# Batch norm with ReLU: the first load of x in four strided parts, and the parameter vectors read through the gpsimd queue

## The chip, the core and the metric

The kernel runs on one core of one Trainium2 chip, written in Bass with the Tile framework. The metric is the device time of one execution in microseconds. The kernel before takes 83.73 us, the median of three runs (83.72 to 83.98).

## The reference

Inference-mode batch normalisation of x with shape (32, 128, 32, 32) in float32, followed by ReLU:

```python
normalized = (x - running_mean[None, :, None, None]) / np.sqrt(running_var[None, :, None, None] + eps)
scaled = normalized * gamma[None, :, None, None] + beta[None, :, None, None]
return np.maximum(scaled, 0).astype(np.float32)
```

x is 16.78 MB and the result is as large. The four parameter vectors have 128 floats each; eps is the constant 1e-5. Since the statistics are given, each channel needs one scale and one bias, and each element one multiply, one add and one maximum.

## The kernel before

**Tiling.** Batch and channel are put together into 4,096 rows of 1,024 floats (one image of one channel, 4 KB). A block t (there are two) is 128 partitions times J = 16 rows: partition p of block t holds rows 2048 t + 16 p to 2048 t + 16 p + 15. So a partition holds 16 neighbouring channels, and scale and bias are tables of 128 x 16. The j-th row of a partition uses column j of these tables.

**Pieces.** Each block is cut along j into pieces (PIECES, line 16): for block 0 rows 0-1, 2-3, 4-7 and 8-15, for block 1 rows 0-7 and 8-15. A piece is one tile of its own and is loaded by one transfer (line 52) of 128 partitions, each of which receives one contiguous stretch of 8, 16 or 32 KB. All pieces have their own buffer; x fits into SBUF whole, and no load waits for a buffer to come free. The six loads are issued by SP (SyncE), in the order of the pieces.

**Parameters.** Four transfers, issued by ACT (line 59), put the four vectors into `raw`, 8 partitions x 4 x 16 floats, 64 bytes per partition and vector. POOL writes a 0/1 matrix `rep` (lines 63 and 64: memset, then affine_select), and one matrix product (line 74) spreads the 8 partitions over 128, into `cols` in PSUM. ACT takes the square root of the variance plus eps (line 82), and DVE makes the reciprocal, the scale and the bias (lines 84 to 90).

**Main loop.** ACT goes through the pieces (lines 93 to 108): for each row j one activation of 128 x 1,024 with ReLU, scale and bias (line 96), in place. After the last row of a piece, and after row 0 of the first piece (STORE_CUTS), ACT issues the store of what is finished (line 104). There are 7 stores: two of 0.5 MB, then 1, 2, 4, 4 and 4 MB.

**What sets the order.** Each engine executes its instructions in the program's order; the main loop's order on ACT is the written one. Transfers issued by SP and by ACT go through one queue each. Tile gives each of these transfers one of eight completion semaphores, in turn, and when a transfer takes over a semaphore that an earlier one used, its issuing engine first waits until the earlier one has landed. In the kernel before, the fourth load of x (rows 8-15 of block 0) takes over the semaphore of running_var, the fifth that of running_mean, and the sixth that of the second piece of x.

Of the kernel before, what the change touches and what calls it, by code (L numbers as in the profile page):

```python
# [1 line left out]

# [4 lines left out]


F32 = mybir.dt.float32
ACTF = mybir.ActivationFunctionType  # L10

J = 16

PIECES = (((0, 2), (2, 4), (4, 8), (8, 16)), ((0, 8), (8, 16)))

STORE_CUTS = {(0, 1)}


@with_exitstack
def kernel(
    ctx: ExitStack,
    tc: tile.TileContext,
    x: bass.AP,
    gamma: bass.AP,
    beta: bass.AP,
    running_mean: bass.AP,
    running_var: bass.AP,
    eps: bass.AP,  # L30
    out: bass.AP,
):
    nc = tc.nc
    B, C, H, W = x.shape
    HW = H * W
    P = nc.NUM_PARTITIONS
    assert C % J == 0 and P % (C // J) == 0 and (B * C) % (P * J) == 0
    Q = C // J
    T = B * C // (P * J)

    xr = x.rearrange("b c h w -> (b c) (h w)").rearrange("(t p j) w -> t p j w", p=P, j=J)
    outr = out.rearrange("b c h w -> (b c) (h w)").rearrange("(t p j) w -> t p j w", p=P, j=J)

    data = ctx.enter_context(tc.tile_pool(name="data", bufs=1))
    params = ctx.enter_context(tc.tile_pool(name="params", bufs=1))
    psum = ctx.enter_context(tc.tile_pool(name="psum", bufs=1, space=bass.MemoryType.PSUM))

    tiles = []
    for t in range(T):
        for a, b in PIECES[t]:  # L50
            xt = data.tile([P, b - a, HW], F32, name=f"x{t}_{a}")
            nc.sync.dma_start(out=xt, in_=xr[t, :, a:b, :])  # L52
            tiles.append((t, a, b, xt))

    raw = params.tile([Q, 4, J], F32, name="raw")
    for k, src in enumerate((running_var, gamma, running_mean, beta)):
        nc.scalar.dma_start(out=raw[:, k, :], in_=src.rearrange("(q j) -> q j", j=J))
    eps_t = params.tile([P, 1], F32, name="eps_t")  # L60
    nc.vector.memset(eps_t, float(eps))  # L61
    rep = params.tile([Q, P // Q, Q], F32, name="rep")
    nc.gpsimd.memset(rep, 1.0)  # L63
    nc.gpsimd.affine_select(  # L64
        out=rep,
        in_=rep,
        compare_op=mybir.AluOpType.is_equal,
        fill=0.0,
        base=0,
        pattern=[[0, P // Q], [-1, Q]],  # L70
        channel_multiplier=1,
    )
    cols = psum.tile([P, 4, J], F32, name="cols")
    nc.tensor.matmul(  # L74
        cols.rearrange("p k j -> p (k j)"),
        rep.rearrange("q r s -> q (r s)"),
        raw.rearrange("q k j -> q (k j)"),
        start=True,
        stop=True,
    )  # L80
    std_t = params.tile([P, J], F32, name="std_t")
    nc.scalar.activation(out=std_t, in_=cols[:, 0, :], func=ACTF.Sqrt, bias=eps_t[:, 0:1], scale=1.0)  # L82
    rstd_t = params.tile([P, J], F32, name="rstd_t")
    nc.vector.reciprocal(out=rstd_t, in_=std_t)  # L84
    scale_t = params.tile([P, J], F32, name="scale_t")
    nc.vector.tensor_mul(out=scale_t, in0=cols[:, 1, :], in1=rstd_t)  # L86
    ms_t = params.tile([P, J], F32, name="ms_t")
    nc.vector.tensor_mul(out=ms_t, in0=cols[:, 2, :], in1=scale_t)  # L88
    bias_t = params.tile([P, J], F32, name="bias_t")
    nc.vector.tensor_sub(out=bias_t, in0=cols[:, 3, :], in1=ms_t)  # L90

    with tc.manual_schedule(engines={mybir.EngineType.Activation}):
        for t, a, b, xt in tiles:
            first = a
            for j in range(a, b):
                nc.scalar.activation(  # L96
                    out=xt[:, j - a, :],
                    in_=xt[:, j - a, :],
                    func=ACTF.Relu,
                    bias=bias_t[:, j : j + 1],  # L100
                    scale=scale_t[:, j : j + 1],
                )
                if j + 1 == b or (t, j + 1) in STORE_CUTS:
                    nc.scalar.dma_start(
                        out=outr[t, :, first : j + 1, :], in_=xt[:, first - a : j + 1 - a, :]
                    )
                    first = j + 1


# [1 line left out]
_INS = ['x', 'gamma', 'beta', 'running_mean', 'running_var', 'eps']  # L111
_OUTS = [((32, 128, 32, 32), 'float32')]

_NUMBERS = {'eps': 1e-05}


# [26 lines left out]
```

## Time and profile before

| what | us |
|---|---|
| median of the runs shown | 83.73 |
| the profiled execution | 83.77 |
| its span, first to last instruction | 81.9 |
| ACT busy in the span (34 instructions) | 38.5 |
| PE, DVE and POOL busy, each | below 1 |
| first ReLU starts | 9.72 |
| last ReLU ends, and the last store is issued | 55.97 |
| load and store packets' time, each, on 16 DMA engines | 48.4% and 47.8% of the span |

The span counts from the core's first instruction to its last. The rest of the execution's time lies before and after it. DMA issues are listed as instructions of the engine that issues them (SPq, ACTq); the time given there is that of the issue, and not that of the transfer, which the DMA engines carry out later. A releaser ("<-") is what ended an engine's idle time. In tables by window, the last columns are the granted TensorE clock, the mean busy share of the 16 DMA engines (it can pass 1, as a packet is counted where it starts), and the GB/s that they moved.

### The profile page before, as it was taken

What the parts mean: (1) busy time and instruction counts of PE and PEld (TensorE: products, weight loads), DVE (VectorE), ACT (ScalarE), POOL (GpSimd) and SP (SyncE); (2) the same over time, 40 slices, a digit from 0 to 9 for tenths busy, and PEclk for the clock granted to TensorE, in tenths of its full rate; (3) what the DMA queues carried; (4) which work ended last, traced back from release to release, by engine and by line L of the source; (5) the groups of instructions that cost most, each with busy time, mean ns of one, the idle gap of its engine ahead of it and who ended that gap; (6) DMA issues with size and microseconds to landing.
All of it is one profiled execution on the core that took longest, in us unless ns stands there. A gap on an engine that the chain in (4) does not pass through costs nothing.

```text
span 81.9 us, 119 instructions
## 1 busy us (share of the span) xinstructions
PE 0.7 (1%) x2; PEld 0.5 (1%) x2; DVE 0.8 (1%) x5; ACT 38.5 (47%) x34; POOL 0.8 (1%) x6
## 2 busy tenths in 40 slices
PE   0002000000000000000000000000000000000000
PEld 0002000000000000000000000000000000000000
DVE  0000300000000000000000000000000000000000
ACT  0600377799039999199994199993000000000000
POOL 3000000000000000000000000000000000000000
DMA  2899999989899999979789798996999899799690
GB/s 32 328 425 472 408 448 448 512 352 494 370 448 416 446 418 396 500 296 600 320 380 580 304 464 384 512 512 288 480 512 400 368 512 448 320 512 496 272 512 0
DMA packets 1936, 33.56 MB, mean 410 GB/s; under 512 B 272, under 2 KB 272, under 8 KB 528
## 3 DMA queue, kind: packets, MB, share of 16 engines
q1 hardware_dynamic: 864, 16.78, 48.4%
q10 hardware_dynamic: 1072, 16.78, 47.8%
HBM read 16.78 MB, written 16.78 MB: 410 GB/s over the span
## 4 chain that ended last, share of the span: by engine, by line
DMA 56%; ACT 11%; SPq 0%; issue 0%
DMA x<-in_x_dram 56%; ACT x L96 11%; SPq L52 0%
## 5 line engine op out<-in xcount | busy, mean ns | idle before, releaser
L96 ACT ACTIVATE x<-x,bias_t,scale_t 128x1024 f32<-128x1024 f32 x32 | 37.0, 1228 | 10.3 <-DMA x<-in_x_dram 7.9
L82 ACT ACT_TABLE_LOAD x1 | 1.3, 1283 | 2.6 <-issue 2.6
L82 ACT ACTIVATE std_t<-cols,eps_t 128x16 f32<-128x16 f32 x1 | 0.3, 273 | 4.5 <-PE cols L74 4.5
L74 PE MATMUL cols<-raw,rep 8*128 8x64 f32 x2 | 0.7, 428 | 7.7 <-DMA raw<-in_beta_dram 7.7
L74 PEld LDWEIGHTS cols<-raw,rep 8*128 8x128 f32 x2 | 0.5, 304 | 7.7 <-issue 7.7
L64 POOL TENSOR_SCALAR_AFFINE_SELECT rep<-rep 8x128 f32<-8x128 f32 x1 | 0.4, 392 | 0.1
L84 DVE RECIPROCAL rstd_t<-std_t 128x16 f32<-128x16 f32 x1 | 0.3, 254 | 7.8 <-ACT std_t L82 7.8
L63 POOL MEMSET rep<- 8x128 f32 x1 | 0.2, 195 | 0.3 <-POOLq L124 0.3
L86 DVE TENSOR_TENSOR scale_t<-cols,rstd_t 128x16 f32<-128x16 f32 x1 | 0.2, 175 | 0.1
L90 DVE TENSOR_TENSOR bias_t<-cols,ms_t 128x16 f32<-128x16 f32 x1 | 0.2, 175 | 0.0
L88 DVE TENSOR_TENSOR ms_t<-cols,scale_t 128x16 f32<-128x16 f32 x1 | 0.2, 175 | 0.0
L124 POOL MEMSET const-bfloat16-1.0<- 128x1 bf16 x1 | 0.1, 106 | 0.0
L124 POOL MEMSET const-uint8-127<- 128x1 uint8 x1 | 0.1, 106 | 0.0
L124 POOL MEMSET const-float32-0.0<- 128x1 f32 x1 | 0.1, 103 | 0.3 <-issue 0.3
L124 POOL MEMSET const-float32-1.0<- 128x1 f32 x1 | 0.1, 103 | 0.0
L61 DVE MEMSET eps_t<- 128x1 f32 x1 | 0.1, 59 | 0.9 <-PEq L124 0.9
## 6 DMA issues: line engine op xcount, KB each, us to landing
x<-in_x_dram SPq DMA_DIRECT2D x3, 4096.0 KB, 38.8
out_dram<-x ACTq DMA_DIRECT2D x3, 4096.0 KB, 27.9
x<-in_x_dram SPq DMA_DIRECT2D x2, 1024.0 KB, 5.7
x<-in_x_dram SPq DMA_DIRECT2D x1, 2048.0 KB, 11.2
out_dram<-x ACTq DMA_DIRECT2D x1, 2048.0 KB
out_dram<-x ACTq DMA_DIRECT2D x2, 512.0 KB, 18.8
out_dram<-x ACTq DMA_DIRECT2D x1, 1024.0 KB
raw<-in_running_var_dram ACTq DMA_DIRECT2D x1, 0.5 KB
```

What stands on the lines that cost most here:

```text
L61: nc.vector.memset(eps_t, float(eps))
L63: nc.gpsimd.memset(rep, 1.0)
L64: nc.gpsimd.affine_select(out=rep, in_=rep, compare_op=mybir.AluOpType.is_equal, fill=0.0, base=0, pattern=[[0, P // Q], [-1, Q]], channel ...
L74: nc.tensor.matmul(cols.rearrange("p k j -> p (k j)"), rep.rearrange("q r s -> q (r s)"), raw.rearrange("q k j -> q (k j)"), start=True, s ...
L82: nc.scalar.activation(out=std_t, in_=cols[:, 0, :], func=ACTF.Sqrt, bias=eps_t[:, 0:1], scale=1.0)
L84: nc.vector.reciprocal(out=rstd_t, in_=std_t)
L86: nc.vector.tensor_mul(out=scale_t, in0=cols[:, 1, :], in1=rstd_t)
L88: nc.vector.tensor_mul(out=ms_t, in0=cols[:, 2, :], in1=scale_t)
L90: nc.vector.tensor_sub(out=bias_t, in0=cols[:, 3, :], in1=ms_t)
L96: nc.scalar.activation(out=xt[:, j - a, :], in_=xt[:, j - a, :], func=ACTF.Relu, bias=bias_t[:, j : j + 1], scale=scale_t[:, j : j + 1],)
L124: nc = _bacc.Bacc("TRN2", target_bir_lowering=False, num_devices=1)
```

## The change

Two things change.

The first piece of x (block 0, rows 0-1) is loaded by four transfers instead of one. Transfer s takes partitions s, s + 4, s + 8 and so on: 32 partitions with 8 KB each. All four write to the same tile, with a semaphore each, and SP issues them one after the other ahead of the other five loads, which are as before. The first ReLU now waits for all four.

The four parameter vectors are read by transfers that POOL (GpSimd) issues instead of ACT. They stand on POOL ahead of the memset and the affine_select that make `rep`, and use completion semaphores of a kind of their own. With the transfers that remain on SP and ACT, the eight semaphores are now handed round differently: the fourth load of x takes over that of the first of the four transfers, the fifth that of the last of the four, and the sixth that of the first store.

```diff
 STORE_CUTS = {(0, 1)}
+
+SEED = 4
...
             xt = data.tile([P, b - a, HW], F32, name=f"x{t}_{a}")
-            nc.sync.dma_start(out=xt, in_=xr[t, :, a:b, :])
+
+            n = SEED if (t, a) == (0, 0) else 1
+            for s in range(n):
+                nc.sync.dma_start(out=xt[s::n], in_=xr[t, s::n, a:b, :])
             tiles.append((t, a, b, xt))
...
     raw = params.tile([Q, 4, J], F32, name="raw")
     for k, src in enumerate((running_var, gamma, running_mean, beta)):
-        nc.scalar.dma_start(out=raw[:, k, :], in_=src.rearrange("(q j) -> q j", j=J))
+        nc.gpsimd.dma_start(out=raw[:, k, :], in_=src.rearrange("(q j) -> q j", j=J))
```

## The prediction

> **What bounds the kernel now.** I read the slices and the queue totals first, then the chain of waits, then the waits of SP's own queue, and last the windows and the timeline of the first microseconds.
>
> ```profile
> DMA  2899999989899999979789798996999899799690
> ACT  0600377799039999199994199993000000000000
> ...
> q1 hardware_dynamic: 864, 16.78, 48.4%
> q10 hardware_dynamic: 1072, 16.78, 47.8%
> ...
> DMA x<-in_x_dram 56%; ACT x L96 11%; SPq L52 0%
> L96 ACT ACTIVATE x<-x,bias_t,scale_t 128x1024 f32<-128x1024 f32 x32 | 37.0, 1228 | 10.3 <-DMA x<-in_x_dram 7.9
> ```
>
> The 16 DMA engines are busy in every slice from the second on, with loads (q1) and stores (q10) taking half each. ACT works 37.0 of 81.9 us, waits for x, and is done long before the end. The chain names loads and ACT only because it is followed from instructions; after its last entry the DMA engines still drain stores. So this is a byte stream of 33.56 MB with a head and a tail.
>
> ```profile
> 0.00:1.50 1.50, 0.00 (x0) 0.00 (x0) 0.06 (x1) 0.00 (x0) 0.80 (x6) 1.00 0.00 0
> 1.80:1.90 0.10, 0.00 (x0) 0.00 (x0) 0.00 (x0) 0.00 (x0) 0.00 (x0) 1.00 2.35 329
> 1.90:2.00 0.10, 0.00 (x0) 0.00 (x0) 0.00 (x0) 0.00 (x0) 0.00 (x0) 1.00 1.60 246
> 2.00:2.50 0.50, 0.00 (x0) 0.00 (x0) 0.00 (x0) 0.00 (x0) 0.00 (x0) 1.00 0.60 131
> 2.50:3.00 0.50, 0.00 (x0) 0.00 (x0) 0.00 (x0) 0.38 (x1) 0.00 (x0) 1.00 0.77 311
> 4.00:5.00 1.00, 0.00 (x0) 0.00 (x0) 0.00 (x0) 0.00 (x0) 0.00 (x0) 1.00 1.01 418
> 60.00:80.00 20.00, 0.00 (x0) 0.00 (x0) 0.00 (x0) 0.00 (x0) 0.00 (x0) 1.00 0.98 421
> 80.30:80.60 0.30, 0.00 (x0) 0.00 (x0) 0.00 (x0) 0.00 (x0) 0.00 (x0) 1.00 0.02 0
> ```
>
> (Windows; the last two columns are the DMA share and GB/s, bytes counted where their packet starts.) x starts at 1.8 us, the flow is even near 420 GB/s from 3 us, with loads alone, mixed, or stores alone, and ends at about 80.45. From 1.8 to 3.0 us, 33 + 25 + 66 + 156 = 280 KB move; at 426 GB/s it would be 511 KB. That lack of 231 KB is 0.54 us of ramp. So the profiled run of 83.77 us is: 1.8 before the first bytes, 0.54 of ramp, 78.1 of stream (33.56 MB at 430 GB/s), 1.45 of completions and closing barrier in the span, 1.87 outside it. It is 0.04 above the median of 83.73, so I carry sums over unchanged.
>
> ```profile
> SPq L52 <- DMA raw<-in_running_mean_dram: 4.1, 1, 4.1
> ...
> 0.81 0.59 ACTq L59 DMA_DIRECT2D raw<-in_running_var_dram  x1
> 1.43 0.29 ACTq L59 DMA_DIRECT2D raw<-in_gamma_dram  x1
> ...
> 10.99 0.38 ACTq L104 DMA_DIRECT2D out_dram<-x  x1
> ```
>
> SP's fifth load waited 4.1 us, since completion semaphores are handed round among eight and it takes over the one of a parameter. While SP and ACT both issue, the first parameter issue takes 0.59 us against 0.29 for the next.
>
> **What the Trainium skill says.** "DMA: Bandwidth & Descriptors", section "Issuing engines are not separate DMA queues": transfers of all issuing engines run on the same 16 DMA engines and interleave. The trace agrees: 418 GB/s with loads alone, 421 with stores alone. Same page, "The descriptor swizzle": in a 128-partition transfer each DMA engine writes the partitions of one SBUF port; for other shapes it only says that the outer size decides how many engines take part. "SBUF — State Buffer", section "Door 1: The DMA port swizzle": four neighbouring partitions share a port, ports repeat after 32, and 1 MiB over 8 ports ran at 189 GB/s against 328 over all 16. "DMA: Bandwidth & Descriptors", "Latency and other measured facts": first byte about 0.6 us from SP or ACT, about 1 us from gpsimd. Here SP's first issue begins at 0.81 and bytes start at 1.8; ports and gpsimd transfers are in no run before.
>
> **The change part by part.**
>
> *Parameters off ACT's queue.* ACT loses four issues (0.59 + 0.29 + 0.31 + 0.45 = 1.64 us), and its table load moves from 2.6 to about 1 us. Nothing waits for that: ACT is next needed when the matmul is done at 8.4. It frees the start for SP: the first parameter's packets stand just ahead of x. Worth 0 to 0.1 us at the head.
>
> *Parameters onto POOL's queue.* Four issues now stand ahead of the memset of rep (0.20 us) and its affine_select (0.39). At an estimated 1 us each, from the skill's first-byte figure, they run from 0.8 to 4.8, and rep, ready at 1.5 before, is ready near 5.6. The tiny packets then take turns with x's rows, as they did before, when the last parameter let the matmul start at 7.73. I put the matmul at 6 to 12 us, so first ReLU at 8 to 14 instead of 9.72. Cost on the end: 0. What hides it is the backlog: loads alone are 16.78 / 0.426 = 39.4 us of DMA work. The cover ends where the last store comes too late: ACT needs 56.31 - 9.72 - 7.9 (its waits for loads) = 38.7 us, the last store of 4.19 MB 9.85 us, so first ReLU may be as late as 80.45 - 9.85 - 38.7 = 31.9.
>
> *The semaphores move along.* The built order shows that in the new kernel the fourth load of x waits for seed 0, the fifth for seed 3, and the sixth (the last) for the first store. That store was issued at 10.99 and landed 14.2 us later, at 25.2; the last load was issued at 7.99 before and will be at about 25 to 30. Queued behind it on SP: nothing but the closing waits. It costs 0, because the fifth load keeps its queue busy until ACT gets it at 34.8: 5 to 9 us of cover; past that, stores of 1 to 4 MB stand in the other queue and the engines stay busy.
>
> *Four transfers for one.* Each moves 32 rows of 8 KB, 2 per DMA engine. SP's issues took 328 to 678 ns, median 398; three more are 1.2 us of SP. Per seed an engine has 2 rows of 8 KB at 418/16 GB/s, 0.63 us of work, so issue keeps ahead and the later loads are still early. 48 more completion packets are 3 per engine: under 0.1 us. At the head, fewer rows are made ready before all 16 engines have one: worth from 0 to the ramp's 0.54 us. I take 0.1, because even with descriptors at hand a first row has to come from HBM, and nothing in the trace says that the ramp is descriptor generation.
>
> *Ports.* This is the term that decides. Every fourth partition reaches all 16 ports, but what counts is which engine takes which rows. If 32 rows are dealt out so that each engine keeps a port of its own, the price is 0. If they are dealt out in plain order, two rows each, engine e takes partitions 8e+s and 8e+4+s, two neighbouring ports, and engine e+4 takes the same two (32 partitions on). Two engines then always work through the same pair of ports in the same order. In step, each gets half: 8 rows x 0.31 us (8 KB at 26 GB/s) = 2.5 us becomes 5.0. Every DMA engine has a fixed share of bytes, so the slowest pair sets the end. Bounds 0 to +2.5. The skill describes the port-by-port deal for 128 partitions only, so I take plain order as likelier, and 2.0 of the 2.5, since engines start up to a row apart and partly miss each other.
>
> Sum: 83.77 + 2.0 (ports) - 0.15 (head) = 85.6.
>
> **The rivals.** (A) Forecast: ports shared while the seeds load; 85.6, own range 84.6 to 86.2. For it: no layout for 32 rows is promised, and the skill's 189 against 328 GB/s says that half the ports carry about half the rate. Against: no run shows it. (B) No change: engines keep a port each, the ramp stays; 83.7, 83.5 to 83.95. For it: everything else hides under the stream. (C) Faster, by one mechanism: the ramp of 0.54 us is the time in which 128 rows' descriptors are made, and 32 rows need a quarter, 0.54 x 3/4 = 0.4 us earlier; 83.35. For it: SP's first issue shares the start with ACT's, and engines begin over 1.8 to 2.5 us. It shows as a gain from 0.25 us, and needs unshared ports. (D) POOL gets slow enough to matter, first ReLU after 31.9: each microsecond beyond costs one; it would take parameters five times later than now.
>
> **How the numbers follow.** A 0.50, B 0.24, C 0.21, D and small losses (issue slower than 0.63 us per seed, closing work for the gpsimd queue) 0.05, near 84.1. About 0.3%, 0.25 us, is what a measurement here can tell from none. Faster 0.21, same 0.24, slower 0.55. The range is 83.2 to 86.2: C down to its likely end, A up to full sharing with the head gained; outside it lie the full ramp gain and sharing that spreads to the second load.
>
> **What would show it.** Right: x's first piece lands about 2 us later (at 5.5 us before: 4.7, the shortest landing of an x load, after its issue at 0.81), the GB/s between 2 and 7 us near 210 to 300 instead of 420, then the same stream, ending 2 us later; first ReLU anywhere from 8 to 14 us without moving the end; SP's last load issued near 25 to 30 us. Wrong: 420 GB/s from 2.5 or 3 us on would mean ports are not shared, and the time is B's or C's by where the ramp begins; holes in the slices between 35 and 80 us would mean that a store or the late load does matter.

## The result, and the profile after

The changed kernel takes 86.69 us (median; 86.44 to 87.24), the kernel before beside it 83.77. The ratio is 1.0347, 95% interval 1.0314 to 1.0380: 2.9 us slower, where 1.9 us were forecast and 2.4 us was the upper end of the range. The profiled execution took 86.67 us with a span of 85.0, which is 3.1 more than before.

The slices and queue totals of the kernel after, from its page:

```profile
DMA  0989999999999999999999899999999999999950
GB/s 0 294 274 355 420 417 501 411 417 417 417 411 442 417 447 422 415 419 459 432 436 440 378 428 478 455 432 417 447 432 432 447 417 432 447 432 417 432 216 0
...
q1 hardware_dynamic: 912, 16.78, 48.0%
q10 hardware_dynamic: 1008, 16.78, 46.0%
...
L101 ACT ACTIVATE x<-x,bias_t,scale_t 128x1024 f32<-128x1024 f32 x32 | 37.0, 1228 | 13.2 <-DMA x<-in_x_dram 10.9
```

The same bytes in the same two queues, the same 37.0 us of activations: still a byte stream. What is new stands at the ends of the second row. Slices of 2.1 us carry 294, 274 and 355 GB/s before the stream reaches 420, and the slice before last carries 216. In between it runs as before.

Windows show it more finely. The kernel after (last two columns: mean busy share of the DMA engines, GB/s):

```profile
2.00:3.00 1.00, 0.00 (x0) 0.00 (x0) 0.00 (x0) 0.31 (x1) 1.00 (x3) 1.00 0.87 246
3.00:4.00 1.00, 0.00 (x0) 0.00 (x0) 0.00 (x0) 0.00 (x0) 0.93 (x4) 1.00 1.01 345
4.00:6.00 2.00, 0.00 (x0) 0.00 (x0) 0.00 (x0) 0.00 (x0) 0.19 (x1) 1.00 0.78 246
6.00:10.00 4.00, 0.66 (x2) 0.50 (x2) 0.18 (x1) 0.27 (x1) 0.00 (x0) 1.00 1.03 377
80.00:81.00 1.00, 0.00 (x0) 0.00 (x0) 0.00 (x0) 0.00 (x0) 0.00 (x0) 1.00 0.99 426
81.00:82.00 1.00, 0.00 (x0) 0.00 (x0) 0.00 (x0) 0.00 (x0) 0.00 (x0) 1.00 0.69 295
82.00:83.00 1.00, 0.00 (x0) 0.00 (x0) 0.00 (x0) 0.00 (x0) 0.00 (x0) 1.00 0.08 33
```

The same windows of the kernel before:

```profile
2.00:3.00 1.00, 0.00 (x0) 0.00 (x0) 0.00 (x0) 0.38 (x1) 0.00 (x0) 1.00 0.69 221
3.00:4.00 1.00, 0.00 (x0) 0.00 (x0) 0.00 (x0) 0.90 (x1) 0.00 (x0) 1.00 1.01 426
4.00:6.00 2.00, 0.00 (x0) 0.00 (x0) 0.00 (x0) 0.00 (x0) 0.00 (x0) 1.00 1.01 418
6.00:10.00 4.00, 0.65 (x2) 0.49 (x2) 0.78 (x4) 0.55 (x2) 0.00 (x0) 1.00 1.07 455
```

Two things are to be seen. Between 4 and 6 us the engines move 246 GB/s instead of 418, and their busy share is 0.78: they are partly *idle*. Engines that share ports would be busy at a low rate (e6 below shows that picture), so the forecast's mechanism is in doubt from this line on. And the end is ragged: the share falls from 0.99 over 0.69 to 0.08 within three microseconds, so the engines no longer finish together.

The trace also holds a record of each DMA packet: its queue, start, duration and bytes, but not its engine. A packet of x carries one partition's contiguous stretch, called a row from here on. Each load and store ends with 16 packets of 4 bytes, read here as one completion mark per engine (96 for the six loads of the kernel before).

These records give both sizes. By the marks of the last store, the stream is 1.89 us behind that of the kernel before when it ends, on the mean of the 16 engines (82.32 us against 80.43), and the last engine ends 1.41 us after that mean (83.73), against 0.18 before (80.61). So 1.89 us of lag and 1.23 us of straggling make the 3.1 us of span.

The lag is made in the first 10 us: counted in bytes it is 0.25 us at 4 us, 1.08 at 6 and 1.70 at 10, and from 16 us on it stays between 1.8 and 2.0. From 4 to 10 us the mean engine is idle for 0.33 us, nearly all of it before 6 us, and slow rows take 0.9 us per engine more than their normal time. So the slow rows are the larger part, and more than half of that time (0.57 us) belongs to rows begun after 6 us, when the engines hardly idle any more.

The straggling begins at the head, too. For the piece of rows 4-7 the engines put down their completion marks over 2.5 us (13.4 to 15.9), for the piece of 4 MB after it again over 2.5 us (24.5 to 26.9), and they end over 2.1 us. Before, the first two of these spreads are 0.3 and 0.4 us. A spread that arose in the first microseconds is still there at the last store. That it is the same engine throughout is likely, but the records don't show it.

The issues of x by SP, up to 4.4 us (shortest, median, longest in ns). Before, then after:

```profile
L52 SPq DMA_DIRECT2D x<-in_x_dram x4: 372/426/678, 0.8 to 2.2; - x4
```

```profile
L57 SPq DMA_DIRECT2D x<-in_x_dram x6: 432/578/594, 0.8 to 3.9; - x6
```

A strided seed costs SP 0.54 to 0.59 us instead of about 0.42, so one goes out every 0.62 us. A seed is 0.62 us of work for the 16 engines (two rows of 8 KB each at 0.309 us). The queue gets its next work just when the last is done, and nothing is in hand. The first row of x begins at 2.13 us instead of 1.84.

The parameters' side, in the timeline of the kernel after:

```profile
1.33 0.67 POOL L64 DMA_DIRECT2D raw<-in_running_var_dram  x1 [0.81 <-POOLq L129]
...
3.01 0.52 POOL L64 DMA_DIRECT2D raw<-in_beta_dram  x1
3.52 0.20 POOL L68 MEMSET rep<- 8x128 f32 x1
3.79 0.40 POOL L69 TENSOR_SCALAR_AFFINE_SELECT rep<-rep 8x128 f32<-8x128 f32 x1
...
10.81 1.24 ACT L101 ACTIVATE x<-x,bias_t,scale_t 128x1024 f32<-128x1024 f32 x1 [1.02 <-DVE bias_t L95]
```

and SP's waits:

```profile
SPq L57 <- DMA out_dram<-x: 17.9, 1, 17.9
SPq L57 <- DMA x<-in_x_dram: 4.0, 1, 4.0
```

POOL issues the four in 0.67 + 3 x 0.52 us and has `rep` ready at 4.2. The matrix product then waits for the last parameter, which lands at 8.7, and the first ReLU starts at 10.81. SP's last load waits 17.9 us for the first store, is issued at 27.1, and no slice between 35 and 80 us is low.

### The profile page after: what moved, and what is told of

Its sections match the earlier page's. It is cut to its first block, busy times and chain, and to the rows that moved or that the text cites. A ratio compares the mean times of both kernels' runs of the same rounds, so it can differ in the third digit from the quotient of the medians.

```text
span 85.0 us, 123 instructions
## 1 busy us (share of the span) xinstructions
PE 0.7 (1%) x2; PEld 0.5 (1%) x2; DVE 0.8 (1%) x5; ACT 38.5 (45%) x34; POOL 3.0 (4%) x10
## 4 chain that ended last, share of the span: by engine, by line
DMA 52%; ACT 11%; issue 3%; POOL 2%; DVE 1%; PE 1%; DVEq 0%; POOLq 0%
DMA x<-in_x_dram 28%; DMA out_dram<-x 18%; ACT x L101 11%; DMA raw<-in_beta_dram 7%; POOL raw L64 2%; PE cols L79 1%; ACT std_t L87 0%; DVE rstd_t L89 0%; DVE ms_t L93 0%; DVE scale_t L91 0%; DVE bias_t L95 0%; DVEq L91 0%; POOLq L129 0%
## 5 line engine op out<-in xcount | busy, mean ns | idle before, releaser
L64 POOL DMA_DIRECT2D raw<-in_running_var_dram x1 | 0.7, 672 | 0.8 <-POOLq L129 0.8
L64 POOL DMA_DIRECT2D raw<-in_gamma_dram x1 | 0.5, 518 | 0.0
L64 POOL DMA_DIRECT2D raw<-in_running_mean_dram x1 | 0.5, 518 | 0.0
L64 POOL DMA_DIRECT2D raw<-in_beta_dram x1 | 0.5, 518 | 0.0
```

The source lines that it names most:

```text
L64: nc.gpsimd.dma_start(out=raw[:, k, :], in_=src.rearrange("(q j) -> q j", j=J))
```

## The experiments

Theories at the outset. *Ports*: two engines share a port pair while seeds load, and each row takes up to twice as long. *Supply*: the seeds come too slowly or too small for one queue, engines run dry, and rows take their normal time. *Parameters*: the gpsimd queue and the later first store have a price. In most kernels below the four parameter reads are left out and `raw` is filled with constants, so that only the loads of x differ; this is called "no parameter reads". Its edit is the first one shown. All ratios are to the kernel before on the same chip, with the 95% interval.

### No parameter reads, first piece whole (e1)

```diff
-    for k, src in enumerate((running_var, gamma, running_mean, beta)):
-        nc.scalar.dma_start(out=raw[:, k, :], in_=src.rearrange("(q j) -> q j", j=J))
+    nc.vector.memset(raw[:, 0:2, :], 1.0)
+    nc.vector.memset(raw[:, 2:4, :], 0.0)
```

> The kernel before without any parameter transfer: raw is filled with ones (variance, gamma) and zeros (mean, beta) by DVE, so the reading of the four vectors is left out. It is the base for the two other kernels without parameter transfers. Three theories stand against each other for the loss of 2.9 us. Ports: two DMA engines share SBUF ports in a strided transfer of 32 partitions, which so runs at about half the rate. Issue: such a transfer takes SP longer to issue (0.54 to 0.59 us in the changed kernel against 0.37 to 0.43), and the engines run out of rows. Gpsimd: the parameter transfers of POOL hold up the DMA engines or SP's issues. All three expect 83.4 to 83.9 us here, as the parameters are hidden.

84.12 us, 1.0032 (1.0020 to 1.0043). It is the base for the kernels below, and by itself a surprise: without any parameter transfer, and with the first ReLU at 5.71 us instead of 9.72, it is not faster but 0.3% slower. The packet records put the loss at 9 to 12 us (0.3 us) and 40 to 50 us (0.2 us), where loads and earlier stores mix and some rows are slow; the start is as before.

### The four seeds alone (e2), and the gpsimd queue alone (e3)

e2 is e1 with the change's four strided transfers:

```diff
-            nc.sync.dma_start(out=xt, in_=xr[t, :, a:b, :])
+            n = SEED if (t, a) == (0, 0) else 1
+            for s in range(n):
+                nc.sync.dma_start(out=xt[s::n], in_=xr[t, s::n, a:b, :])
```

e3 is the kernel before with the other half of the change:

```diff
-        nc.scalar.dma_start(out=raw[:, k, :], in_=src.rearrange("(q j) -> q j", j=J))
+        nc.gpsimd.dma_start(out=raw[:, k, :], in_=src.rearrange("(q j) -> q j", j=J))
```

> The first piece in four strided transfers, and no parameter transfer at all (raw filled by DVE as in the base, the reading of the four vectors is left out). Ports and issue: 2 to 3 us above the base, 85.7 to 86.8. Gpsimd: within 0.3 us of the base, 83.4 to 84.0. If SP's issues are slow because of their shape they still take 0.54 to 0.59 us; if POOL made them slow they take 0.33 to 0.43.

> The kernel before with the second half of the change alone: parameters read by the gpsimd queue, the first piece in one transfer. Ports and issue: no change, 83.5 to 84.0. Gpsimd: most of the loss, 85.2 to 86.7, with SP's first issues at 0.54 us or more and fewer than 16 engines busy between 4 and 6 us.

e2: 86.49 us, 1.0313 (1.0288 to 1.0337), or 2.81% over e1. e3: 84.36 us, 1.0055 (1.0030 to 1.0079), above the range without a price (83.5 to 84.0) and far under that of the gpsimd theory. The two add up to 3.36% against the change's 3.47%, well inside its interval. So about five sixths of the loss belong to the seeds. The windows of e2 repeat the pattern of the kernel after, though POOL issues nothing here:

```profile
4.00:6.00 2.00, 0.00 (x0) 0.00 (x0) 0.00 (x0) 0.00 (x0) 0.00 (x0) 1.00 0.79 258
6.00:10.00 4.00, 0.00 (x0) 0.00 (x0) 0.00 (x0) 1.38 (x2) 0.00 (x0) 1.00 1.01 346
```

Share 0.79, so idle engines again. Of the 22 rows of 8 KB that began between 3.5 and 4.0 us, 15 took 0.309 us, the time of an undisturbed row; ports shared by pairs of engines would show in all of them. The slowest rows (0.7 to 1.2 us) come from 4 us on, beside the idling and for two microseconds after it.

### Strided transfers where the queue is full (e5)

e2's edit, moved from the first piece to the 4 MB piece of rows 8-15 of block 0 (the condition is `(t, a) == (0, 8)`); the first piece is whole. The seeds have the same 32 partitions, with 32 KB each.

> No parameter transfer (raw filled by DVE, the reading of the four vectors is left out), the first piece whole, and instead the piece of rows 8 to 15 of block 0 (4.19 MB) in four strided transfers of 32 partitions with 32 KB each. SP issues them while the engines still have the pieces before to load, and each holds 2.5 us of work. Ports: these 4.19 MB run at half the rate, 9.8 us become up to 19.7, and the time is 88 to 94. Issue: within 0.5 us of the base, 83.4 to 84.3. Gpsimd: the same as issue.

84.01 us, 1.0024 (1.0016 to 1.0033): not slower than e1. In the stretch in which most of these rows are loaded it moved

```profile
12.00:25.00 13.00, 0.00 (x0) 0.00 (x0) 0.00 (x0) 4.63 (x4) 0.00 (x0) 1.00 1.06 452
```

and e1, with the whole transfer,

```profile
12.00:25.00 13.00, 0.00 (x0) 0.00 (x0) 0.00 (x0) 4.79 (x5) 0.00 (x0) 1.00 1.02 438
```

If every fourth partition made engines share ports, these 4 MB, 9.8 us of work at 426 GB/s, would take up to twice as long. They run at full rate: all 128 rows of 32 KB took 1.21 us, the time of such rows in the kernel before. The ports theory falls for strided seeds. SP's last load goes out only at 27.7 us here, as late as in the changed kernel, so that lateness isn't the loss either.

### Neighbouring partitions instead (e6)

As e2, with transfer s taking the 32 neighbouring partitions from 32 s on.

```diff
-                nc.sync.dma_start(out=xt[s::n], in_=xr[t, s::n, a:b, :])
+                q = P // n
+                nc.sync.dma_start(out=xt[s * q : s * q + q], in_=xr[t, s * q : s * q + q, a:b, :])
```

> No parameter transfers (raw filled by DVE; the reading of the four vectors is left out), the first piece in four transfers of 32 neighbouring partitions, 0 to 31, 32 to 63 and so on. Three theories for the 2.4 us that the four strided transfers cost without any parameter transfer. Supply: SP hands out one of them every 0.62 us, just what 16 engines load in that time (2 rows of 8 KB each), so engines run out of rows, and a row that starts on an idle engine takes 0.5 to 1 us instead of 0.31. Deal: rows of a strided transfer are dealt out so that engines get in each other's way, and the packets are slow for that. Count: three more small transfers cost by themselves, whatever their shape. Supply: SP's issues show whether the stride makes them slow: 85.8 to 86.8 if they still take 0.53 to 0.59 us, 83.9 to 84.6 if they take 0.43 or less. Deal: another time, 88 or more if neighbours make it worse, under 84.6 if better. Count: as the strided ones, 86.2 to 86.8.

85.36 us, 1.0169 (1.0143 to 1.0195), outside all the ranges: SP's issues were fast (0.38 to 0.43 us), but there is another cost. Here the ports do show:

```profile
3.00:4.00 1.00, 0.00 (x0) 0.00 (x0) 0.52 (x3) 0.00 (x0) 0.00 (x0) 1.00 1.05 229
4.00:6.00 2.00, 0.00 (x0) 0.00 (x0) 0.00 (x0) 0.00 (x0) 0.00 (x0) 1.00 1.08 238
```

The engines are busy throughout (share 1.05 to 1.08) and move 229 to 238 GB/s. All 13 rows that began between 3.5 and 4.0 us took 0.62 to 0.64 us, twice 0.309. The Trainium skill ("SBUF — State Buffer", "Door 1: The DMA port swizzle") says that 32 neighbouring partitions reach 8 of 16 ports, with 189 against 328 GB/s for 1 MiB; that is a ratio of 0.58, and the trace's 0.56 (238 of 426) agrees. This is what a shared port looks like. Such a doubling of every row isn't in the traces of the change.

### All partitions, a quarter of the columns each (e7)

As e2, with transfers of 128 partitions and 2 KB:

```diff
-            for s in range(n):
-                nc.sync.dma_start(out=xt[s::n], in_=xr[t, s::n, a:b, :])
+            if n > 1:
+                for s in range(n):
+                    j, c = s // 2, (s % 2) * (HW // 2)
+                    nc.sync.dma_start(out=xt[:, j, c : c + HW // 2], in_=xr[t, :, j, c : c + HW // 2])
+            else:
+                nc.sync.dma_start(out=xt, in_=xr[t, :, a:b, :])
```

> No parameter transfers (raw filled by DVE; the reading of the four vectors is left out), the first piece in four transfers of all 128 partitions with 2 KB each: the same 256 KB per transfer, in the shape of a whole load. Supply: issues of 0.37 to 0.43 us every 0.47 us stay ahead of 0.62 us of work, 83.9 to 84.6. Deal: no loss, 83.9 to 84.4. Count: 86 to 86.8.

85.35 us, 1.0168 (1.0127 to 1.0209). No stride, no shared port. SP's issues are fast, and the first row begins at 1.80:

```profile
L59 SPq DMA_DIRECT2D x<-in_x_dram x4: 366/422/432, 0.8 to 2.2; - x4
```

They go out every 0.47 us for 0.67 us of work each (per engine eight rows of 2 KB at 0.084 us). Yet the engines run dry at the same place:

```profile
4.00:6.00 2.00, 0.00 (x0) 0.00 (x0) 0.00 (x0) 1.24 (x1) 0.00 (x0) 1.00 0.89 286
```

So slow issue is not the whole cause, and the supply theory as it stood (83.9 to 84.6) missed: four transfers of 256 KB on one queue lose 1.1 us (1.36% over e1) even when SP is ahead. Slow rows stand beside the idling here too, although these transfers have no stride.

### A bigger first piece (e8), and seeds on two queues (e9)

e8 makes the first piece of four rows instead of two (PIECES of block 0: 0-3, 4-7, 8-15), so each strided seed has 1.2 us of work. e9 is e2 with every other seed issued by ACT:

```diff
-                nc.sync.dma_start(out=xt[s::n], in_=xr[t, s::n, a:b, :])
+                (nc.sync if s % 2 == 0 else nc.scalar).dma_start(out=xt[s::n], in_=xr[t, s::n, a:b, :])
```

> No parameter transfers (raw filled by DVE; the reading of the four vectors is left out), block 0 in pieces of 4, 4 and 8 rows, and the first, of 2.1 MB, in four strided transfers of 32 partitions with 16 KB each. A transfer now holds 1.23 us of work for 0.62 us of SP. Supply: the loss is gone but for the later head, 0.3 us: 84.2 to 84.9. Deal: at least the loss of the smaller ones, as twice the bytes are dealt out in the bad way: 86.3 to 89. Count: as the smaller ones, 86.2 to 86.8.

> No parameter transfers (raw filled by DVE; the reading of the four vectors is left out), the first piece in the four strided transfers of the change, but two issued by SP and two by ACT at the same time. Supply: if SP's instruction is what takes the time, two queues halve it and the loss falls to under 1 us, 84.2 to 85.2; if both share what makes the rows ready, issues take 0.8 us and more and the loss stays. Deal and count: as with SP alone, 86.2 to 86.8.

e8: 85.18 us, 1.0151 (1.0114 to 1.0188), above the 84.2 to 84.9 of the supply theory. Idle time between 4 and 6 us falls from 0.38 us (e2) to 0.07. The run has no partner with a whole first piece of four rows, so what the larger piece does by itself is not separated. e9: 84.67 us, 1.0112 (1.0053 to 1.0171), two thirds of e2's loss over e1 gone (2.81% to 0.80%). Its window:

```profile
4.00:6.00 2.00, 0.00 (x0) 0.00 (x0) 0.71 (x4) 0.00 (x0) 0.00 (x0) 1.00 0.99 410
6.00:10.00 4.00, 0.00 (x0) 0.00 (x0) 0.00 (x0) 2.93 (x3) 0.00 (x0) 1.00 1.05 440
```

Same transfers, same bytes, two queues: no idling, and the first ReLU starts at 6.22 us instead of 8.17.

### The second piece in seeds (e10)

e2's edit with the condition `(t, a) == (0, 2)`: the first piece is whole, the second of the same size is in four strided seeds.

> No parameter transfers (raw filled by DVE; the reading of the four vectors is left out); the first piece whole, and the second, of the same size, in four strided transfers of 32 partitions with 8 KB each. Theory refill: a queue brings a new transfer's rows to the engines only some 0.8 us after the one before, and that costs only when no rows are queued ahead; at the start of the kernel none are. Here the first piece covers the engines until 4.9 us, and the four transfers are issued by 3.6 us: no loss, 83.9 to 84.4 (the base had 84.12), no idle engines between 4 and 8 us. Rival small: transfers of 256 KB cost about 0.6 us each wherever they stand: 86 to 86.8.

84.62 us, 1.0080 (1.0053 to 1.0106), 0.48% over e1 where e2 is 2.81%:

```profile
4.00:6.00 2.00, 0.00 (x0) 0.00 (x0) 0.00 (x0) 0.34 (x1) 0.00 (x0) 1.00 1.02 406
```

One megabyte queued ahead keeps the engines fed while the seeds are issued. Most of the price is for small transfers at the *very start*, with an empty queue. The rest, not foreseen (83.9 to 84.4), comes with slow rows and no idle engines: slow rows don't need a pause.

### A later first ReLU by itself (e11)

The kernel before, with two activations on a scratch tile ahead of the first ReLU, on ACT:

```diff
+    pad = params.tile([P, 2, HW], F32, name="pad")
+    nc.vector.memset(pad, 0.0)
...
+        for i in range(2):
+            nc.scalar.activation(
+                out=pad[:, i, :],
+                in_=pad[:, i, :],
+                func=ACTF.Relu,
+                bias=bias_t[:, 0:1],
+                scale=scale_t[:, 0:1],
+            )
```

> The kernel before, with two activations of 128 x 1,024 on a scratch tile ahead of the first ReLU, so that the first ReLU and the first store come about 2.4 us later, as they do with the parameters on the gpsimd queue (11.97 instead of 9.72 us). If the 0.5% that this half of the change cost alone comes from where the stores meet the loads, it shows here too: 84.1 to 84.6. If it comes from the gpsimd transfers themselves, there is no change: 83.6 to 83.95.

84.36 us, 1.0059 (1.0044 to 1.0074), the same as e3's 1.0055. The first ReLU here and in e3 (timelines):

```profile
11.68 1.23 ACT L107 ACTIVATE x<-x,bias_t,scale_t 128x1024 f32<-128x1024 f32 x1
```

```profile
11.97 1.24 ACT L96 ACTIVATE x<-x,bias_t,scale_t 128x1024 f32<-128x1024 f32 x1 [1.02 <-DVE bias_t L90]
```

Both are 2.0 to 2.3 us later than before (9.72), and both lose half a microsecond. So the price of the gpsimd half, taken alone, is that of the later stores; nothing has to be charged to the gpsimd queue itself. By the packet records most of the lag is gathered between 35 and 50 us, where the later, still mixed, loads and stores have slow rows: 0.59 us per engine in e3 and 0.42 in e11 from 35 to 45 us, 0.04 before. Why those rows are slow was not tried.

### The whole change on two queues (e12), and two strided halves (e13)

e12 is the changed kernel with e9's edit. e13 is e2 with SEED = 2: two transfers of every second partition, 1.2 us of work each.

> The changed kernel complete, parameters on the gpsimd queue, with transfers 0 and 2 of the four on SP and 1 and 3 on ACT. Refill: two queues bring rows twice as fast, no idle engines and no slow packets between 4 and 10 us; what stays is the later head and up to 0.5 us of the gpsimd half: 84.4 to 85.2. Small, or gpsimd transfers that hold up SP: as the changed kernel, 86.3 to 87.2.

> No parameter transfers (raw filled by DVE; the reading of the four vectors is left out), the first piece in two strided transfers of 64 partitions, 512 KB or 1.23 us of work each. Refill: little is left beside the later head, if a stride makes the first issue slow here too: 84.2 to 85.0. Small: half of the four transfers' loss, 85.1 to 85.6.

e12: 85.27 us, 1.0169 (1.0101 to 1.0237), at the upper end of what was expected (84.4 to 85.2) and half of the change's loss; e9's 1.12% and the gpsimd half's 0.55% make 1.67%. e13: 85.26 us, 1.0170 (1.0139 to 1.0201). e13's engines do not idle between 4 and 6 us, but it is 0.5 us behind the kernel before by 5 us and its last engine ends 0.74 us after the mean. Its time lies in the range of the rival that gives every small transfer a price (85.1 to 85.6), so that rival needed a test.

### Columns on two queues (e14), and two row transfers (e15)

What was left open was why e7 loses with fast issue: the pace of one queue, or a fixed sum for each further transfer. e14 is e7 with the second and fourth transfer issued by ACT. e15 is e1 with the first piece in two transfers of 128 partitions, one image row (4 KB) each, both by SP:

```diff
-                    nc.sync.dma_start(out=xt[:, j, c : c + HW // 2], in_=xr[t, :, j, c : c + HW // 2])
+                    (nc.sync if s % 2 == 0 else nc.scalar).dma_start(out=xt[:, j, c : c + HW // 2], in_=xr[t, :, j, c : c + HW // 2])
```

```diff
+SEED = 2
...
-            nc.sync.dma_start(out=xt, in_=xr[t, :, a:b, :])
+            n = SEED if (t, a) == (0, 0) else 1
+            if n > 1:
+                for s in range(n):
+                    nc.sync.dma_start(out=xt[:, s, :], in_=xr[t, :, s, :])
+            else:
+                nc.sync.dma_start(out=xt, in_=xr[t, :, a:b, :])
```

> Left out: reading the four parameter vectors (raw is filled with constants). The first piece is loaded by four transfers of 128 partitions and 2 KB, the first and third on SP's queue and the second and fourth on ACT's. Theory (one queue can't hand out such small transfers fast enough, even when they are issued quickly): with two queues the idle time of the DMA engines between 4 and 6 us is gone and the time is 83.9 to 84.6 us. Rival (each transfer costs a fixed sum whatever its queue, so that the number of transfers decides): about 85.3 us, as with the four column transfers on one queue.

> Left out: reading the four parameter vectors (raw is filled with constants). The first piece is loaded by two transfers of 128 partitions and 4 KB (one image row each) on SP's queue, so each has 1.23 us of work for the engines. Theory (the queue runs dry where a transfer has less work than the pitch at which the queue takes up the next): no idle time of the engines between 4 and 6 us and 83.9 to 84.6 us. Rival (a fixed sum for each transfer added): about 84.7 us, a third of the way from one transfer to four.

e14: 84.02 us, 1.0031 (1.0018 to 1.0044). e15: 84.19 us, 1.0051 (1.0034 to 1.0067). Windows of e14:

```profile
3.00:4.00 1.00, 0.00 (x0) 0.00 (x0) 0.47 (x3) 0.34 (x2) 0.00 (x0) 1.00 0.97 369
4.00:6.00 2.00, 0.00 (x0) 0.00 (x0) 0.30 (x2) 1.14 (x1) 0.00 (x0) 1.00 1.09 434
```

and of e15:

```profile
4.00:6.00 2.00, 0.00 (x0) 0.00 (x0) 0.00 (x0) 1.12 (x1) 0.00 (x0) 1.00 1.04 420
```

Four transfers on two queues end no later than e1 (1.0032), so a fixed sum for each transfer whatever its queue (85.3 us) is out: e7's 1.1 us at the end is the price of the single queue. Two transfers of twice the size on one queue also lose little (0.2%, the intervals overlap). Splitting isn't free at the head, though. By the packet records e14 is 0.34 us and e15 0.43 us behind the kernel before at 8 us, where e1 isn't behind and e7 is by 1.14. e14 ends level with e1 because e1 falls behind later, by 0.34 us in all, when its stores join the loads.

### All of it in one table

From the packet records: start of the first row of x, idle time of the mean engine from 4 to 6 us, excess time of slow rows per engine for rows begun from 4 to 10 us, and when the engines end. All in us, each from the one profiled execution; the ratio is that of all runs.

| kernel | first row | idle 4-6 | slow rows 4-10 | mean end | last end | ratio |
|---|---|---|---|---|---|---|
| before | 1.84 | 0 | 0.0 | 80.43 | 80.61 | 1 |
| after | 2.13 | 0.33 | 0.9 | 82.32 | 83.73 | 1.0347 |
| e1 whole | 1.80 | 0 | 0.2 | 80.77 | 81.04 | 1.0032 |
| e3 gpsimd only | 1.81 | 0 | 0.0 | 81.00 | 81.29 | 1.0055 |
| e11 later ReLU only | 1.80 | 0 | 0.0 | 80.91 | 81.16 | 1.0059 |
| e2 four strided, one queue | 2.11 | 0.38 | 1.1 | 82.53 | 83.69 | 1.0313 |
| e9 four strided, two queues | 2.14 | 0 | 0.1 | 81.23 | 81.51 | 1.0112 |
| e12 change, two queues | 2.15 | 0.06 | 0.3 | 81.43 | 82.59 | 1.0169 |
| e13 two strided, one queue | 2.14 | 0 | 0.0 | 81.21 | 81.95 | 1.0170 |
| e7 four columns, one queue | 1.80 | 0.34 | 0.9 | 81.67 | 82.73 | 1.0168 |
| e14 four columns, two queues | 1.80 | 0 | 0.0 | 80.84 | 81.07 | 1.0031 |
| e15 two rows, one queue | 1.79 | 0 | 0.1 | 80.94 | 81.33 | 1.0051 |
| e8 four strided of 512 KB, one queue | 2.12 | 0.07 | 0.5 | 81.57 | 81.96 | 1.0151 |
| e6 four quarters, one queue | 1.81 | 0 | 1.5 | 82.16 | 82.60 | 1.0169 |
| e10 second piece strided | 1.80 | 0 | 0.7 | 81.14 | 81.75 | 1.0080 |
| e5 fourth piece strided | 1.81 | 0 | 0.2 | 80.98 | 81.16 | 1.0024 |

Idle time and straggling come together: the three kernels with 0.3 us and more of idling end 1.1 to 1.4 us later on their last engine than on the mean, e9 and e14 0.2 to 0.3. It isn't the only way to a straggler: e12 has 0.06 us of idling and a last engine 1.2 us after the mean. No kernel tried beats the kernel before.

What stays open: what inside a queue sets its pace, since e7's SP is ahead of the engines by its issue times; why rows of 8 KB begun between 4 and 10 us take up to 1.6 us in the changed kernel; and the rest of the strided forms' loss. e9 is 0.8% (0.7 us) above e14 and e13 1.2% (1.0 us) above e15. The later first row doesn't explain this: at 8 us e9 and e14 are 0.31 and 0.34 us behind the kernel before, e13 and e15 0.49 and 0.43. The gap opens between 8 and 12 us, when the first stores begin (0.75 against 0.42 us at 12 us, 0.83 against 0.65), and in the stragglers.

## Why the prediction was wrong

*Direction, place and rate: right by luck, for the wrong reason.* The loss was forecast in the first microseconds, carried unchanged to the end. That is where the lag is made: 282 GB/s from 2 to 7 us (382 before), in the forecast band of 210 to 300, and the seeds had all landed at 8.0 us, where about 7.5 was foretold. But "GB/s" alone did not separate the theories. The DMA share beside it did.

*Step "Ports", 2.0 us: failed.* It rested on plain dealing of rows to engines making pairs of engines share ports. Strided rows kept 0.309 us (e2), and 4 MB in strided seeds cost nothing (e5). So nothing of the 2.0 us shows in this change. The mechanism exists for 32 neighbouring partitions (e6: rows of 0.62 to 0.64 us, 1.15 us over e1), the layout that the change does not use.

*Step "Four transfers for one", "so issue keeps ahead": failed, and this is where the time went.* It took 0.4 us per issue from whole transfers, set it against 0.63 us of work and put both at a price of nothing. A strided issue is 0.54 to 0.59 us, one every 0.62 us for 0.62 us of work, so nothing was ahead; and even with issues every 0.47 us one queue runs dry (e7). The term belongs at 2.35 us (e2 over e1) instead of under 0.1: about 1.1 for four small transfers on one empty queue (e7 over e1) and 1.2 more for the stride (e2 over e7). The second is the difference of two runs; the slow issue is part of the stride, but what makes the whole of it isn't shown. The prediction had named "issue slower than 0.63 us per seed" among the small losses, near 84.1, with 0.05. At most it priced the pause between transfers. It had no term for the slow rows that came with the pause (0.9 us per engine, against 0.33 us of idling), nor for an engine that ends 1.41 us after the mean.

*Step "head", -0.15: wrong sign.* The first row comes 0.3 us later (2.13 against 1.84) in all forms with a strided first piece, and at the same 1.80 us for one whole transfer (e1) and for four of columns (e7). In bytes the changed kernel is only 0.10 us behind at 3 us, so the price of this is small. Rival C's mechanism was not seen: fewer rows per transfer did not shorten the start.

*Step "Parameters onto POOL", 0 on the end: timing right, price wrong at least for this half alone.* First ReLU at 10.81, in the window of 8 to 14. The estimate of 1 us per issue was too high (0.67 and 0.52). But the later stores cost 0.5% in e3, and in e11 without gpsimd, though they were far inside the cover up to 31.9 us. That cover counted bytes and ACT's time; it did not count that the mix of loads and stores in time has a price of its own, which e1, with *earlier* stores, shows from the other side.

*Step "the semaphores move along", 0: no sign against it.* SP's last load was issued at 27.1 us (25 to 30 foretold) after 17.9 us of waiting, and the windows from 35 to 80 us are whole.

Rebuilt with the measured terms, the sum is 83.77 + 2.35 (seeds, e2 over e1) + 0.46 (later stores, e3) = 86.58, against 86.69. That the sum fits doesn't show its last term inside the change. In e3 that lag arises between 35 and 50 us (from 0 to 0.56 us). The changed kernel is 1.93 us behind at 35 us and 1.89 at 50, and e12, with the same gpsimd half, 1.02 and 0.99. Their first stores come 1.1 and 1.2 us later than before, not 2. What this half costs beside the seeds stays open.

## What to carry to other kernels

At this kernel's start the DMA queue is empty, and nothing tried there beat the kernel before with its whole first load. Four pieces of 256 KB on one queue left the engines idle, whether SP issued them every 0.62 us or every 0.47; with room in hand (e10) or on two queues (e14) most of the loss was gone. In a kernel bound by its byte stream, a delay made in the first 10 us was still there at 80. Before a low GB/s is put down to a shared resource, look at the busy share beside it: here idle engines went with a lack of supply, and engines busy at half the rate with shared ports. And the issue time of whole transfers is no price for the issue of a strided one.

## What the hardware showed that was not expected

- At the start, SP's issue depends on the shape: 0.37 to 0.43 us for columns or neighbouring partitions (e6, e7), 0.53 to 0.59 us for every fourth or second partition (e2, e13), and the strided ones put the first row 0.3 us later. Shape isn't all: the fourth whole load before took 0.68 us, and two of the late strided issues in e5 0.47.
- Two queues gave more than the saved issue time. The Trainium skill ("DMA: Bandwidth & Descriptors", "Rules for kernel authors") says that spreading transfers over issuing engines doesn't help bandwidth and only saves issue time. Once the stream runs, nothing here speaks against it; at the start, the same four column transfers took 85.35 us on one queue and 84.02 on two (1.0168 and 1.0031), although the single queue's issues were ahead of the work.
- Seeds of every fourth partition, 32 in all, run at full row rate, while 32 neighbouring ones take twice the time per row.
- Shifting the first store either way cost time: 2 us later 0.5% (e3, e11), and 4 us earlier 0.3% (e1, where the parameter reads are gone as well). At 1.1 us later, the changed kernel shows no such lag.
